# Row-factor root, rotary steps and weight sums reordered in front of the attention loop of a hybrid decoder block

## The chip, the cores and the metric

The kernel runs on one core of a Trainium2 chip. That core has five engines with a queue of instructions each: TensorE (PE) for matrix products, VectorE (DVE) and ScalarE (ACT) for element-wise work, GpSimd (POOL) for element-wise work on the core's own memory and for issuing transfers, and SyncE (SP) for issuing transfers. An engine takes its instructions in the order of its queue; the engines meet at semaphores. PE writes to the accumulator memory PSUM, which is divided into banks.

The metric is the device time of one execution in microseconds (us), from the first to the last work of the program; lower is better.

## The reference

One layer on x of 1024 rows by 1024 channels, all in float32. An RMS norm is followed by a projection into a pooling input u (512), 8 query heads and 2 key/value heads of 64, and two gates of 1024. The first 16 channels of each query and key head are rotated by position. Attention runs in blocks of 128 rows over the block itself and the one before, with a window of 128 and one sink logit per head. A multi-scale average pooling with its own mixing is the other branch. Both go through branch weights, are gated and added, and an output projection, a norm and a squared-ReLU MLP follow.

```python
h = _rmsnorm(x, g_mix_pre[l])
proj = jnp.einsum('bsd,de->bse', h, w_in[l]) + b_in[l]
u_pool, q, k, v, gates = jnp.split(proj, IN_SPLITS, axis=-1)
y_pool = _multiscale_pool(u_pool, w_pool[l], pool_scale[l])
q = _partial_rotary(q.reshape(B, S, N_Q_HEADS, HEAD_DIM), cos, sin)
k = _partial_rotary(k.reshape(B, S, N_KV_HEADS, HEAD_DIM), cos, sin)
...
y_attn = _sliding_window_sink_attention(q.reshape(...), k, v, attn_sinks[l])
merged = (g_pool * jnp.einsum('bsc,cd->bsd', y_pool, w_branch_pool[l])
          + g_attn * jnp.einsum('bsc,cd->bsd', y_attn, w_branch_attn[l]))
mix = jnp.einsum('bsd,de->bse', merged, w_out[l])
x = x + _rmsnorm(mix, g_mix_post[l])
```

## The kernel before

**Number format.** Every float32 operand of a product is split into a high part (a rounding copy, mostly on ACT, L101) and a low part (the difference, on DVE, L104); a product is three matmuls, high by high, high by low and low by high. So each operand costs one ACT and one DVE instruction before PE can use it whole.

**The front.** Channels lie on partitions and the 1024 rows are cut into two halves of 512 (`th` 0 and 1). The six groups of 128 projected channels are f = 0 to 3 (queries with 32 value channels each) and f = 4, 5 (the first 80 partitions hold the channels to be rotated, in two halves; the rest keys that are not). For each of 8 slices k of the input channels, `scaled` multiplies x by the norm's gain (high part on ACT at L202, low on DVE at L203), and `mm_in` (L187) adds three matmuls. The norm's factor per row, r1, comes from sums of squares: `square_row` (and L967 for the second half) squares a tile of rows on ACT and sums along it into `ssq`; `factors` takes a root on ACT and a Newton step on DVE through `rsqrt` and spreads the result (L218); `make_rb` transposes it on PE (L224) and copies it as the row `rb` (L225). `close_in` multiplies a finished projection by `rb` on DVE (L353) and adds its bias on ACT (L354). The buffers of the closed second half are those of the first, so the close at f = 4 waits until the first half's rows have been copied out.

**Rotation.** `turn` multiplies the 80 rows by a cosine and a sine table (two instructions of 80x1024, L363), `turn_end` takes their difference and sum (L367, L368), and `rows_in`, `keys_rest` and `values_out` send the rows by small transfers to where queries, keys and values need them, over the queues of SP, ACT and POOL. The first half's rotation runs on DVE, the second's on POOL, in `second_half`, which is what `closing` holds and `flush(closing)` runs.

**Attention.** For each block n of 128 rows: `split_q` makes the query operands (`qt`), `score_all` the scores in two groups of heads (L456) with a copy on ACT (L458), `score_prev` masks them on DVE (L465), `softmax_max` takes maxima (L472 to L474), `softmax_exp` eight exponentials on ACT (L480, L482), `softmax_scale` divides on DVE (L486 to L488), `attend_t` transposes the probabilities on PE (L499) and splits them, `attend_own` masks a copy on DVE (L508), and `attend_v` multiplies by the values (L524) and copies the result (`yt`, L526). Scores, transposes and outputs share two double banks ("sc"), so each waits until the one before last has been read.

**The filler.** The order on PE, DVE and ACT is the order of the program text. Between the steps of attention `fill(t)` takes steps from a stream (`others`) of products that have nothing to do with the block: first 48 steps of the second half's projection (8 for each f), then 16 half products of the gates (L643) of four steps each, with four products of branch weights (`wb_mm`, L780) of two steps in between. A step is three matmuls and is counted as 3 x 0.227 us. `fill` keeps what it has overdrawn and takes whole steps. What the stream needs (splits of gate weights, `load_wb`'s scaled branch weights at L765 on ACT and L768 on DVE) is put on the other engines when the stream reaches certain steps, through the lists `between`, `due` and `lazy`; so where `fill` stands also decides where those instructions stand on ACT and DVE. The stream ends with block 7; whatever the fills took earlier is not there later.

**Weight sums.** `presum(h)` forms sums of parts of the attention branch's weights on DVE, two instructions of 128x512 at each of its two calls (L309, L310; then L305, L306), and stores them for a later stage.

Lines in this text and in the prediction are those of the kernel before, if not said otherwise; the order of the changed kernel shows its own line numbers, which are up to 13 higher (10 in most cases).

Of the kernel before, what the change touches and what calls it, by code (L numbers as in the profile page):

```python
# [8 lines left out]
F32 = mybir.dt.float32  # L9
F32R = mybir.dt.float32r  # L10
# [40 lines left out]
def block_kernel(ctx: ExitStack, tc, xt, x, consts, vecs, sinks, rot, g_post, g_mlp, g_mlp_post,  # L51
# [152 lines left out]

    ssq = sp.tile([P, 20 * NT], F32, name="ssq", bufs=1)[:, :NT]

# [5 lines left out]
    tv = bcp.tile([P, 1024], F32, tag="bc", name="tv")  # L212

    def factors(th):
        n = slice(4 * th, 4 * th + 4)
        rsqrt(r1[:, n], ssq[:, n], 4)
        t = rows_of[th] = at("s4", 4, [2, 512])[:, 0, :]
        dve.tensor_copy(t.rearrange("p (n k) -> p n k", k=P), r1[:, n].unsqueeze(2).broadcast_to([P, 4, P]))  # L218
# [16 lines left out]
    with tc.manual_schedule(engines={mybir.EngineType.PE}):  # L235
# [40 lines left out]
        for n in range(4):  # L276
            square_row(n, at("qkv", 3, [S]) if n < 3 else at("s4", 4, [S]))
        load_table(0)
        factors(0)
        for k in range(NK):  # L280
            if k % 2 == 0:
                xs = flat(yy.tile([P, 2, 512], F32, tag="y", name=nm("xs")))
            nc.sync.dma_start(xs[:, k % 2 * 512:(k % 2 + 1) * 512], xt[k][:, 512:])
            if k < 4:
                scaled(k, 1, xs[:, k % 2 * 512:(k % 2 + 1) * 512])
            else:
                x_late.append((k, 1, xs[:, k % 2 * 512:(k % 2 + 1) * 512]))
# [69 lines left out]

    def turn(th, eng):

        t, tab = raw_r[th][:NR], tables.pop(th)  # L360
        turned[th] = [at("s4", 4, [2, 512])[:NR] for _ in range(2)]
        for i, o in enumerate(turned[th]):
            eng.tensor_tensor(o, t, tab[:NR, i, :].unsqueeze(1).broadcast_to([NR, 2, 512]), ALU.mult)  # L363
# [53 lines left out]
    def second_half(f):  # L417
        close_in(f, 1)
        if f == 5:
            keys_rest(nc.gpsimd, 1)  # L420
            turn(1, pool)
            turn_end(1, pool)
            rows_in(nc.gpsimd, 1, raw_k[1], 4)
        elif f < 4:
            values_out(nc.gpsimd, 1, f)
# [526 lines left out]
    with tc.manual_schedule(engines={mybir.EngineType.PE, mybir.EngineType.DVE, mybir.EngineType.Activation}):  # L952
# [5 lines left out]
        close_in(5, 0)  # L958
        scaled(*x_late[0])
        turn(0, dve)  # L960
        keys_rest(nc.sync, 0)
        for x_ in x_late[1:]:
            scaled(*x_)
        turn_end(0, dve)
        rows_in(nc.sync, 0, raw_k[0], 4)
        for n in range(4, NT):
            act.activation(squares_late[n], squares_late[n], AF.Square, accum_out=ssq[:, n:n + 1])  # L967
        for m in range(4):
            close_in(m, 0)
        factors(1)  # L970
        for m, q in enumerate((nc.sync, nc.sync, nc.scalar, nc.gpsimd)):
            rows_in(q, 0, raw_of(m, 0), m)
        for m in range(4):
            values_out(nc.gpsimd, 0, m)
        load_table(1)
        fill(8.8)
        make_rb(1)
        ready[0] = True
        act.activation(warm, r1[:, :1], AF.Exp)
        flush(closing)  # L980
        presum(0)
        presum(0)
        dve.tensor_scalar(nsnk, snk, -1.0, None, ALU.mult)
        split_k(0)
        fill(3.4)
        split_q(0)
        fill(1.4)
        score_all(0)
        act.activation(tv[:, :512], tv[:, :512], AF.Identity, bias=vec[:, V_BV:V_BV + 1])
        score_prev(0, 0)  # L990
        score_prev(0, 1)
        softmax_max(0)
        split_q(1)
        fill(2.2)
        post_v(0)
        wps = stage([4, P])
        nc.sync.dma_start(wps, w_pool)
        presum_load(1)
        softmax_exp(0, range(3))
# [8 lines left out]
        softmax_max(1)  # L1008
        wpt = yy.tile([P, 2, 4, P], F32R, tag="y", name="wpt")
        split(wpt[:, 0], wpt[:, 1], wps)  # L1010
        wpts.append(wpt)
        fill(3.7)
        for n in range(NT):
            attend_t(n)
            attend_own(n)
            if n == 0:
                presum(1)
            flush(due[0])
# [1507 lines left out]
```

## Time and profile before

| | us |
|---|---|
| three runs, median (lowest to highest) | 1109.07 (1108.18 to 1109.65) |
| the profiled execution's own time | 1108.53 |
| its span, first to last instruction | 1106.7 |
| TensorE busy | 1082.6 (98%) |
| VectorE busy | 901.2 (81%) |
| ScalarE busy | 647.1 (58%) |
| GpSimd busy | 111.2 (10%) |
| mean granted TensorE clock | 0.992 of full |

The profile is of one execution. The span is divided into stretches in which different engines set the pace, and the shares above are means over all of them. In rows of the timeline the columns are start, length, engine, line, operation, output and inputs by the program's names, shapes and count; a bracket at the end is idle time just before, with the instruction that ended it. "PE" are matmuls, "ACTq" is ScalarE's queue when it issues a transfer. Between 0 and about 39 us PE works through the first half's projection, from there to about 183 us through filler and attention, and behind it through gates, branches, output projection and MLP.

### The profile page before, as it was taken

What the parts mean: (1) busy time and instruction counts of PE and PEld (TensorE: products, weight loads), DVE (VectorE), ACT (ScalarE), POOL (GpSimd) and SP (SyncE); (2) the same over time, 40 slices, a digit from 0 to 9 for tenths busy, and PEclk for the clock granted to TensorE, in tenths of its full rate; (3) what the DMA queues carried; (4) which work ended last, traced back from release to release, by engine and by line L of the source; (5) the groups of instructions that cost most, each with busy time, mean ns of one, the idle gap of its engine ahead of it and who ended that gap; (6) DMA issues with size and microseconds to landing.
All of it is one profiled execution on the core that took longest, in us unless ns stands there. A gap on an engine that the chain in (4) does not pass through costs nothing.

```text
span 1106.7 us, 14808 instructions
## 1 busy us (share of the span) xinstructions
PE 1082.6 (98%) x5247; PEld 904.6 (82%) x5247; DVE 901.2 (81%) x1300; ACT 647.1 (58%) x1084; POOL 111.2 (10%) x170
## 2 busy tenths in 40 slices
PE   9997899999999999999999999999999999999997
PEld 7776677888888888888888888888888899899886
DVE  5687789999979787879987976766666899899997
ACT  6757686656665226777765655555544375265653
POOL 0155332200000001100000000100100000000000
PEclk9999899999999999999999999999999999999999
DMA  8747769967994876833276855564898777549842
GB/s 296 230 129 200 201 168 273 295 205 248 298 266 143 232 224 133 237 126 133 96 265 248 292 187 196 182 229 159 279 402 276 240 247 269 169 154 340 296 151 76
DMA packets 107657, 243.30 MB, mean 220 GB/s; under 512 B 10816, under 2 KB 28480, under 8 KB 107584
## 3 DMA queue, kind: packets, MB, share of 16 engines
q1 hardware_dynamic: 86576, 191.76, 51.0%
q0 software_dynamic: 15040, 30.48, 11.5%
q10 hardware_dynamic: 5968, 20.12, 4.7%
q8 instruction: 41, 0.67, 0.2%
q14 instruction: 32, 0.26, 0.1%
HBM read 166.30 MB, written 73.40 MB: 217 GB/s over the span
## 4 chain that ended last, share of the span: by engine, by line
PE 82%; DVE 5%; ACT 3%; issue 2%; DMA 1%; POOL 0%; DVEq 0%; SPq 0%; ACTq 0%
PE mm L643 24%; PE at L643 16%; PE at L2211 12%; PE mm L2211 5%; PE mm L1605 5%; PE at L2185 4%; PE mm L2185 4%; PE mm L554 3%; PE at L1605 2%; PE at L1333 2%; PE mm L1333 1%; PE mm L556 1%; PE sc L524 1%; DVE s L508 1%; ACT s L482 1%
## 5 line engine op out<-in xcount | busy, mean ns | idle before, releaser
L2211 PE MATMUL at<-ar,wh 128*128 128x512 f32 x564 | 134.6, 389 | 0.0
L2211 PEld LDWEIGHTS at<-ar,wh 128*128 128x128 f32 x564 | 105.8, 188 | 22.2 <-DVE ar L104 0.3
L104 DVE TENSOR_TENSOR wh<-st,wh 128x512 fp32r<-128x512 f32 (+1 forms) x106 | 76.3, 731 | 29.7 <-ACT wh L101 27.1
L101 ACT CAST wh<-raw 128x1024 fp32r<-128x1024 f32 (+1 forms) x54 | 53.3, 988 | 79.8 <-PE at L2211 51.9
L643 PE MATMUL mm<-T,wx 128*128 128x512 f32 x375 | 90.6, 389 | 0.0
L104 DVE TENSOR_TENSOR wh<-raw,wh 128x1024 fp32r<-128x1024 f32 (+1 forms) x54 | 61.7, 1142 | 29.6 <-ACT wh L101 29.1
L643 PEld LDWEIGHTS mm<-T,wx 128*128 128x128 f32 x375 | 70.3, 188 | 14.8 <-DVE wx L104 0.2
L101 ACT CAST wh<-st 128x512 fp32r<-128x512 f32 (+2 forms) x105 | 67.6, 653 | 17.7 <-DVE st L599 5.8
L643 PE MATMUL mm<-gr,wh 128*128 128x512 f32 x321 | 77.4, 391 | 0.0
L643 PEld LDWEIGHTS mm<-gr,wh 128*128 128x128 f32 x321 | 59.9, 188 | 12.1
L2211 PE MATMUL mm<-ar,wh 128*128 128x512 f32 x276 | 69.5, 389 | 0.0
L643 PE MATMUL mm<-T,wh 128*128 128x512 f32 x267 | 66.0, 389 | 0.0
L643 PE MATMUL mm<-x,wh 128*128 128x512 f32 x240 | 60.8, 402 | 2.0 <-DVE wh L104 1.2
L101 ACT CAST ar<-B 128x1024 fp32r<-128x1024 f32 (+2 forms) x59 | 43.0, 757 | 30.7 <-PE mm L2211 14.8
L2211 PEld LDWEIGHTS mm<-ar,wh 128*128 128x128 f32 x276 | 51.8, 188 | 10.7
L643 PE MATMUL at<-gr,wh 128*128 128x512 f32 x243 | 59.1, 390 | 0.1
L643 PEld LDWEIGHTS mm<-T,wh 128*128 128x128 f32 x267 | 50.1, 188 | 10.4
L643 PEld LDWEIGHTS mm<-x,wh 128*128 128x128 f32 x240 | 45.6, 194 | 12.8 <-DVE wh L104 1.6
L643 PEld LDWEIGHTS at<-gr,wh 128*128 128x128 f32 x243 | 45.5, 188 | 9.9 <-ACT g L651 0.5
L643 PE MATMUL at<-T,wx 128*128 128x512 f32 x213 | 52.2, 389 | 0.0
L104 DVE TENSOR_TENSOR ar<-B,ar 128x1024 fp32r<-128x1024 f32 (+2 forms) x59 | 49.1, 857 | 1.1 <-ACT ar L101 1.1
L2185 PE MATMUL at<-ar,wh 128*128 128x256 f32 x336 | 47.5, 283 | 0.0
(565 smaller groups left out, 2491.3 us busy)
## 6 DMA issues: line engine op xcount, KB each, us to landing
raw<-f_dram SPq DMA_DIRECT2D x40, 512.0 KB, 4.0
B<-in_w_dn_dram SPq DMA_DIRECT2D x32, 512.0 KB, 6.9
st<-in_w_up_dram SPq DMA_DIRECT2D x27, 512.0 KB, 4.5
f_dram<-g SPq DMA_DIRECT2D x21, 512.0 KB, 3.2
wh<-f_dram SPq DMA_DIRECT2D x20, 512.0 KB, 4.3
g<-spill_dram SPq DMA_DIRECT2D x17, 512.0 KB, 6.6
st<-in_w_g_dram SPq DMA_DIRECT2D x16, 512.0 KB, 4.4
f_dram<-g ACTq DMA_DIRECT2D x16, 512.0 KB, 2.6
```

What stands on the lines that cost most here:

```text
L101: act.copy(hi, src)
L104: return eng.tensor_tensor(lo, src, f32(hi), ALU.subtract)
L482: act.activation(s8[:, h], s8[:, h], AF.Exp, scale=SCALE, bias=nmx[:, h:h + 1], accum_out=den[:, h:h + 1])
L508: dve.tensor_tensor(t, f32(s), own_t.unsqueeze(1).broadcast_to([P, NH, P]), ALU.mult)
L524: pe.matmul(yb[:, kv], v[:, c:c + P], p[ph][:, 4 * kv:4 * kv + 4].rearrange("p i q -> p (i q)"), start=j < 2, stop=j >= len(mms) - 2)
L554: pe.matmul(bs[th], whi[:, k, :], rhs(k, hl, th), start=k == 0 and hl == 0, stop=False)
L556: pe.matmul(bs[th], wlo[:, k, :], rhs(k, 0, th), start=False, stop=k == nk - 1)
L643: pe.matmul(b, w[wh][:, kt, :], x_, start=not after and kt == 0 and j == 0, stop=kt == 3 and j == 2, skip_group_check=after)
L1333: pe.matmul(b, w[wh][:, kt, :], xo[xh][:, kt, :], start=not after and kt == 0 and j == 0, stop=kt == 1 and j == 2, skip_group_check=after)
L1605: pe.matmul(bs[t], Am[a][k][ah][:, t * P:(t + 1) * P], Wm[w][k][wh], start=not after and k == 0 and j == 0, stop=k == 3 and j == 2, skip_g ...
L2185: pe.matmul(part[q][:, t, :], o[fs][fh][:, fk, t * P:(t + 1) * P], o[ws][wh][:, wk, :], start=q not in onto and (s_, t, j) == (0, 0, 0), s ...
L2211: pe.matmul(bs[t], fo[fh][:, k2, t * P:(t + 1) * P], wo_[wh][:, k2, :], start=not after and s2 == 0 and k2 == 0 and j == 0, stop=(s2, k2) ...
```

## The change

Five things are done, all between 36 us and the loop over the blocks:

- The root of the row factors is taken out of `rsqrt` into `root(th)`, which stands right behind the squares on ACT; `factors` keeps the Newton step on DVE. For the second half `factors(1)` now stands behind the four closes and the row transfers. (`ssq` gives up some of its unused room.)
- In the front six instead of four `scaled` of the second half come ahead of `make_rb(0)`. The first rotation's second multiply goes from DVE to POOL.
- The second rotation leaves `second_half` and POOL: `turn(1, dve, dve)`, `turn_end(1, dve)` and `rows_in` stand behind block 0's `softmax_max`, together with the split of `w_pool`, which stood ahead of the loop.
- Both calls of `presum(0)`, the Exp table's warm-up and the sink's negation come ahead of the first `fill`; `split_k(0)` comes ahead of `flush(closing)`; `presum(1)`'s first call moves from block 0 in the loop to the end of the front.
- The fills in front of the loop are 10.8 and 4.3 where there were 8.8, 3.4 and 1.4.

```diff
+    def root(th):
+        roots[th] = small(4, "root")
+        act.activation(roots[th], ssq[:, 4 * th:4 * th + 4], AF.Sqrt, scale=1.0 / D, bias=eps)
...
     def factors(th):
         n = slice(4 * th, 4 * th + 4)
-        rsqrt(r1[:, n], ssq[:, n], 4)
+        ms, r, t = (small()[:, :4] for _ in range(3))
+        dve.tensor_scalar(ms, ssq[:, n], 1.0 / D, EPS, ALU.mult, ALU.add)
+        dve.reciprocal(r, roots.pop(th))
...
         load_table(0)
+        root(0)
         factors(0)
...
-            if k < 4:
+            if k < 6:
                 scaled(k, 1, xs[:, k % 2 * 512:(k % 2 + 1) * 512])
...
         if f == 5:
             keys_rest(nc.gpsimd, 1)
-            turn(1, pool)
-            turn_end(1, pool)
-            rows_in(nc.gpsimd, 1, raw_k[1], 4)
...
-        scaled(*x_late[0])
-        turn(0, dve)
+        turn(0, dve, pool)
         keys_rest(nc.sync, 0)
-        for x_ in x_late[1:]:
+        for x_ in x_late:
             scaled(*x_)
         turn_end(0, dve)
         rows_in(nc.sync, 0, raw_k[0], 4)
         for n in range(4, NT):
             act.activation(squares_late[n], squares_late[n], AF.Square, accum_out=ssq[:, n:n + 1])
+        root(1)
         for m in range(4):
             close_in(m, 0)
-        factors(1)
...
+        factors(1)
         load_table(1)
-        fill(8.8)
+        presum(0)
+        presum(0)
+        act.activation(warm, r1[:, :1], AF.Exp)
+        dve.tensor_scalar(nsnk, snk, -1.0, None, ALU.mult)
+        fill(10.8)
         make_rb(1)
         ready[0] = True
-        act.activation(warm, r1[:, :1], AF.Exp)
+        split_k(0)
         flush(closing)
-        presum(0)
-        presum(0)
-        dve.tensor_scalar(nsnk, snk, -1.0, None, ALU.mult)
-        split_k(0)
-        fill(3.4)
         split_q(0)
-        fill(1.4)
+        wps = stage([4, P])
+        nc.sync.dma_start(wps, w_pool)
+        presum_load(1)
+        fill(4.3)
         score_all(0)
...
         softmax_max(0)
+        wpt = yy.tile([P, 2, 4, P], F32R, tag="y", name="wpt")
+        split(wpt[:, 0], wpt[:, 1], wps)
+        wpts.append(wpt)
+        turn(1, dve, dve)
+        turn_end(1, dve)
+        rows_in(nc.gpsimd, 1, raw_k[1], 4)
         split_q(1)
...
         softmax_max(1)
-        wpt = yy.tile([P, 2, 4, P], F32R, tag="y", name="wpt")
-        split(wpt[:, 0], wpt[:, 1], wps)
-        wpts.append(wpt)
+        presum(1)
         fill(3.7)
         for n in range(NT):
             attend_t(n)
             attend_own(n)
-            if n == 0:
-                presum(1)
             flush(due[0])
```

More of the change, by code (lines that the diff above doesn't have):

```diff
@@ L203, in scaled @@
         dve.scalar_tensor_tensor(t[:, 1, a:b], xs[:, a:b], gk, f32(t[:, 0, a:b]), ALU.mult, ALU.subtract)
-    ssq = sp.tile([P, 20 * NT], F32, name="ssq", bufs=1)[:, :NT]
+    ssq = sp.tile([P, 17 * NT], F32, name="ssq", bufs=1)[:, :NT]
     def square_row(n, t):
@@ L212, in block_kernel @@
     tv = bcp.tile([P, 1024], F32, tag="bc", name="tv")
+    roots = {}
+    def root(th):
+        roots[th] = small(4, "root")
+        act.activation(roots[th], ssq[:, 4 * th:4 * th + 4], AF.Sqrt, scale=1.0 / D, bias=eps)
     def factors(th):
         n = slice(4 * th, 4 * th + 4)
-        rsqrt(r1[:, n], ssq[:, n], 4)
+        ms, r, t = (small()[:, :4] for _ in range(3))
+        dve.tensor_scalar(ms, ssq[:, n], 1.0 / D, EPS, ALU.mult, ALU.add)
+        dve.reciprocal(r, roots.pop(th))
+        dve.tensor_tensor(t, r, r, ALU.mult)
+        dve.tensor_tensor(t, t, ms, ALU.mult)
+        dve.tensor_scalar(t, t, -0.5, 1.5, ALU.mult, ALU.add)
+        dve.tensor_tensor(r1[:, n], r, t, ALU.mult)
         t = rows_of[th] = at("s4", 4, [2, 512])[:, 0, :]
@@ L356, in block_kernel, with turn @@
     turned, raw_k = {}, {}
-    def turn(th, eng):
+    def turn(th, *engs):
         t, tab = raw_r[th][:NR], tables.pop(th)
         turned[th] = [at("s4", 4, [2, 512])[:NR] for _ in range(2)]
-        for i, o in enumerate(turned[th]):
+        for i, (o, eng) in enumerate(zip(turned[th], engs)):
             eng.tensor_tensor(o, t, tab[:NR, i, :].unsqueeze(1).broadcast_to([NR, 2, 512]), ALU.mult)
@@ L995, in block_kernel @@
         post_v(0)
-        wps = stage([4, P])
-        nc.sync.dma_start(wps, w_pool)
-        presum_load(1)
         softmax_exp(0, range(3))
```

## The prediction

> **What bounds the kernel now.** The page comes first, with the busy time of each engine and its share of the span of 1106.7 us.
>
> ```profile
> PE 1082.6 (98%) x5247; PEld 904.6 (82%) x5247; DVE 901.2 (81%) x1300; ACT 647.1 (58%) x1084; POOL 111.2 (10%) x170
> ```
>
> TensorE (PE) works 98% of the span, so only its idle time can be won, and that is not spread evenly. Next the stretches (start:end, then length, busy time of PE, its weight loads, VectorE, ScalarE, GpSimd, granted clock, DMA share, GB/s):
>
> ```profile
> 30.00:60.00 30.00, 26.01 (x132) 20.71 (x131) 20.54 (x42) 19.91 (x36) 4.49 (x9) 0.98 0.70 228
> 60.00:90.00 30.00, 26.32 (x149) 20.51 (x148) 24.21 (x34) 17.04 (x56) 20.24 (x31) 0.96 0.40 114
> 90.00:130.00 40.00, 34.10 (x175) 26.60 (x174) 28.43 (x42) 27.01 (x77) 15.33 (x24) 0.91 0.78 219
> 130.00:183.00 53.00, 50.56 (x280) 40.14 (x279) 48.69 (x65) 44.10 (x114) 18.81 (x31) 0.99 0.75 201
> 183.00:1107.00 924.00, 916.67 (x4391) 772.78 (x4389) 764.52 (x1092) 519.77 (x770) 51.04 (x69) 1.00 0.67 222
> ```
>
> The idle of 30 to 183 us is 3.99 + 3.68 + 5.90 + 2.44 = 16.0 us; all that the diff touches lies there. Behind 183 us PE is full up to its last matmul, so what has shifted by then shifts the end. Who PE waited for (total us, times, longest):
>
> ```profile
> PE mm L780 <- ACT wh L765: 2.8, 1, 2.8
> PE mm L224 <- DVE s L218: 1.8, 1, 1.8
> PE sc L456 <- DVE klo L104: 1.5, 1, 1.5
> PE sc L456 <- DVE qt L104: 1.4, 3, 0.6
> PE mm L187 <- DVE x L203: 0.7, 1, 0.7
> ```
>
> The change aims at L203, L224 and L104's klo: 0.7 + 1.8 + 1.5 = 4.0 us in front of the loop. The waits in the loop, L780 above all, are not touched by a line of the diff, but by its order.
>
> The marks that I measure by are starts on PE: filler of the second half, first scores, transposes of block 0 and of block 1, the second gate half's low weights, the first L780 product's low half, a plain run of filler, the last transposes, and the first matmul behind the loop.
>
> ```profile
> 38.73 3.79 PE L187 MATMUL mm<-x,wkv 128*128 128x512 f32 x16
> 57.54 0.33 PE L456 MATMUL sc<-klo,qt 64*128 64x128 f32 x2 [1.46 <-DVE klo L104]
> 74.11 1.06 PE L499 MATMUL sc<-cst,s 128*128 128x128 f32 x8 [0.36 <-DVE s L488]
> 88.56 1.09 PE L499 MATMUL sc<-cst,s 128*128 128x128 f32 x8 [1.85 <-DVE s L465]
> 97.19 1.20 PE L643 MATMUL mm<-x,wh 128*128 128x512 f32 x4 [1.17 <-DVE wh L104]
> 114.51 2.07 PE L780 MATMUL mm<-wh,wpt 128*128 128x512 f32 x4 [1.11 <-DVE wh L768]
> 150.26 5.72 PE L643 MATMUL mm<-x,wh 128*128 128x512 f32 x24
> 176.15 1.03 PE L499 MATMUL sc<-cst,s 128*128 128x128 f32 x8
> 182.80 3.40 PE L643 MATMUL mm<-x,wh 128*128 128x512 f32 x9
> ```
>
> A filler step is three matmuls: 24 in 5.72 us make 0.7 us a step (0.68 by the kernel's own figure).
>
> **The change part by part.** Prices of VectorE (DVE), in order: two multiplies of the first rotation, one of its sums, two masked copies and a maximum's scaling beside GpSimd, q's two low parts beside GpSimd, the copies alone, a maximum and its scaling alone, one weight sum (a projection's close has its width, 128x512), and a weight's low part that waited for ACT.
>
> ```profile
> 40.16 2.35 DVE L363 TENSOR_TENSOR s<-qkv,s 80x1024 f32<-80x1024 f32 x2
> 45.02 0.69 DVE L368 TENSOR_TENSOR qkv<-s,s 80x512 f32<-80x512 f32 x1
> 59.93 3.54 DVE L465 COPY_PREDICATED s<-cst,pad 128x512 f32<-128x512 uint32 x2 [1.26 <-ACT s L458]
> 64.76 0.96 DVE L473 SCALAR_TENSOR_TENSOR nmx<-nmx,nsnk 128x8 f32<-128x8 f32 x1
> 65.88 1.84 DVE L104 TENSOR_TENSOR qt<-qkv,qt 128x256 fp32r<-128x256 f32 x2
> 69.58 1.37 DVE L465 COPY_PREDICATED s<-cst,sc 128x512 f32<-128x512 uint32 x2 [1.26 <-ACT s L458]
> 73.89 1.21 DVE L472 TENSOR_REDUCE nmx<-s 128x8 f32<-128x1024 f32 x1
> 75.13 0.17 DVE L473 SCALAR_TENSOR_TENSOR nmx<-nmx,nsnk 128x8 f32<-128x8 f32 x1
> 77.51 0.68 DVE L309 TENSOR_TENSOR st<-st,st 128x512 f32<-128x512 f32 x1
> 85.84 0.69 DVE L104 TENSOR_TENSOR wh<-st,wh 128x512 fp32r<-128x512 f32 x1 [2.22 <-ACT wh L101]
> ```
>
> And GpSimd's two multiplies of the second rotation:
>
> ```profile
> 60.33 5.37 POOL L363 TENSOR_TENSOR s<-qkv,s 80x1024 f32<-80x1024 f32 x2
> ```
>
> ScalarE (ACT): row copies issued, `rb` copied, the Exp table, block 0's cast, the copy of its attention output, a branch weight scaled.
>
> ```profile
> 48.98 1.87 ACTq L375 DMA_DIRECT2D qkv<-qkv  x2
> 51.31 0.58 ACT L225 COPY rb_all<-mm 128x512 f32<-128x512 f32 x1 [2.22 <-PE mm L224]
> 51.91 1.28 ACT L979 ACT_TABLE_LOAD   x1
> 75.25 1.01 ACT L101 CAST s<-sc 128x1024 fp32r<-128x1024 f32 x1 [2.63 <-POOL dv L104]
> 83.69 0.99 ACT L526 COPY yt<-sc 128x1024 f32<-128x1024 f32 x1
> 111.47 1.15 ACT L765 ACTIVATE wh<-st,vec 128x1024 fp32r<-128x1024 f32 x1
> ```
>
> *In front of the first scores.* Two `scaled` go ahead of the wait for `rb`, where ACT and DVE stand idle: the 0.7 goes. Half of the first rotation goes to GpSimd at 5.37 / 2 = 2.7 us or a little less, since the two rows of L465 show DVE and GpSimd delaying each other; DVE saves 2.35 / 2 = 1.2, waits, and is done with L368 about 0.7 earlier (45.0 for 45.7). The root behind the squares takes its wait out of `factors`, so the row factors are ready at about 49; sixteen steps of filler from 38.73 end at 49.7, and the 1.8 goes. But `rb` doesn't come earlier: ACT ends its row copies at 50.85 - 0.7 = 50.1, and now loads the table and warms it up (1.28 + 0.2) before it copies `rb`: 51.6 to 52.2, where before had 51.9. Then the keys are split ahead of the closes: 0.6 on ACT (the width of L225), 0.7 on DVE, a close on DVE and two on ACT (0.7 + 1.2), the first of q's casts of half the width (0.3), 0.3 for hand-overs: first scores at about 56.0, 1.5 earlier. PE has 16 + 7 steps done at 54.9, three more than before had, and waits 1.1 there.
>
> *The second rotation on DVE.* It costs 2.35 + 2 x 0.69 = 3.7 us. It saves 3.54 - 1.37 = 2.2 and 0.96 - 0.17 = 0.8 that the two engines took from each other, and 1.84 - 2 x 0.35 = 1.1 at q's low parts (half the width of a 0.69), which stood beside GpSimd's sums: 4.1 together. So it pays for itself, little more; the 1.5 is left and block 0's transposes start at about 72.7, when its probabilities are scaled, with two more steps of filler done.
>
> *The weight sums.* Here the order decides. ACT before, from the eight transposes' neighbours on (q is the projection that is closed, s_119 block 0's probabilities):
>
> ```order
> L407 COPY tv<-mm_759 128x128
> L101 CAST wpt<-st_691 128x512
> L101 CAST s_119_802<-sc_804 128x1024
> L480 ACTIVATE es_773<-es_773 128x8
> L482 ACTIVATE s_107_717,den_774<-s_107_717,nmx_772 128x128 x8
> ```
>
> ACT now, at the same place:
>
> ```order
> L420 COPY tv<-mm_771 128x128
> L367 ACTIVATE q_716<-q_716,vec 128x512
> L101 CAST s_119_816<-sc_818 128x1024
> L490 ACTIVATE es_785<-es_785 128x8
> L492 ACTIVATE s_107_729,den_786<-s_107_729,nmx_784 128x128 x8
> ```
>
> A close of ACT, which needs DVE's close, has come ahead of the cast. DVE before, from block 0's scaling on:
>
> ```order
> L488 TENSOR_TENSOR s_93_629<-s_93_629,den_663 128x1024
> L472 TENSOR_REDUCE nmx_772<-s_107_717 128x8
> L473 SCALAR_TENSOR_TENSOR nmx_772<-nmx_772,nsnk 128x8
> L474 TENSOR_TENSOR es_773<-snk,nmx_772 128x8
> L104 TENSOR_TENSOR wpt<-st_691,wpt 128x512
> L104 TENSOR_TENSOR s_120_803<-sc_804,s_119_802 128x1024
> ```
>
> And now:
>
> ```order
> L498 TENSOR_TENSOR s_94_637<-s_94_637,den_671 128x1024
> L482 TENSOR_REDUCE nmx_784<-s_107_729 128x8
> L483 SCALAR_TENSOR_TENSOR nmx_784<-nmx_784,nsnk 128x8
> L484 TENSOR_TENSOR es_785<-snk,nmx_784 128x8
> L322 TENSOR_TENSOR st_610<-st_609,st_610 128x512
> L323 TENSOR_TENSOR st_609<-st_609 128x512
> L366 TENSOR_TENSOR q_716<-mm_695,rb_all 128x512
> L104 TENSOR_TENSOR s_120_817<-sc_818,s_119_816 128x1024
> ```
>
> That close stands behind the maximum (1.21 + 2 x 0.17 = 1.6) and the two sums (1.4), and the low part of wpt has gone to an earlier place. The cast starts at 72.7 + 1.6 + 1.4 + 0.7 + 0.6 = 77.0 instead of 75.25, 1.75 later. Queued behind it on ACT are block 1's exponentials, q's casts, the next close and a weight's cast, and only then block 0's output copy, which frees the bank of the second half of block 2's scores: 83.69 + 1.75 + 0.6 (the weight's cast, which stood behind it) = 86.0. PE waits some 3 us there. DVE gives the 1.75 back, because it had 2.22 to wait at L104's low part (85.84): block 2's masked copies, block 1's transposes (88.56) and the second half's low weights (97.19) come when they came before. The lead is gone.
>
> *The filler.* `fill` in front of the loop grows from 22.7 to 24.2, two steps. At 97.2 both kernels have done the same filler, but the new one has two steps more to do before block 3's scores: 2 x 0.68 = 1.4 later, and with them the chain of ACT and DVE up to L768: the product at about 115.9. PE idles for it, so behind it the two steps count again: 1.4. Two more waits come from scaled branch weights (ACT 1.15 each) that now stand ahead of a block's score copies. The scores themselves take PE, by the chain,
>
> ```profile
> 120.96 1.65 PE sc L456 x20
> ```
>
> From block 2's last attention product on, ACT has the output copy (0.9), the weight (1.15), a cast (0.6), the first score copy (0.5), and DVE the masked copy (0.7): 3.9 with hand-overs 4.1. PE has two steps (1.4), block 4's scores (1.65) and no more filler ahead of block 3's transposes: a wait of about 1.0. At block 6 DVE's half of the weight stands in the way too (1.2, as ACT's), and PE has a step more (0.7): about 1.0 again, taking 0.5 off for work of ACT that is done by then. On the other side the two longer waits for q's low parts (1.0 of the 1.4) find their cover. At the end, PE before:
>
> ```order
> L643 MATMUL mm_1871<-x_335,wh_1749 128x512 x3
> L499 MATMUL sc_1893<-cst,s_278_1702 128x128 x8
> L780 MATMUL mm_1911<-wh_1821,wpt 128x512 x2
> L780 MATMUL mm_1911<-wh_1822,wpt 128x512
> L780 MATMUL mm_1912<-wh_1821,wpt 128x512 x2
> L780 MATMUL mm_1912<-wh_1822,wpt 128x512
> L524 MATMUL sc_1931<-s_310_1891,v_1575 128x512 x2
> ```
>
> And now:
>
> ```order
> L653 MATMUL mm_1871<-x_335,wh_1749 128x512 x3
> L790 MATMUL mm_1890<-wh_1821,wpt 128x512 x2
> L790 MATMUL mm_1890<-wh_1822,wpt 128x512
> L790 MATMUL mm_1891<-wh_1821,wpt 128x512 x2
> L790 MATMUL mm_1891<-wh_1822,wpt 128x512
> L509 MATMUL sc_1907<-cst,s_281_1715 128x128 x8
> L534 MATMUL sc_1931<-s_313_1905,v_1594 128x512 x2
> ```
>
> The last two steps (L790) have moved ahead of the last transposes, which nothing covers now. From those to 182.80 lies 6.65 us of cast, split and masks, and it stays; so the end moves as the last transposes do.
>
> *Sum.* 0 (lead given back) + 1.4 + 1.4 + 1.0 + 1.0 - 1.0 = 3.8 us. The profiled execution took 1108.5 (1106.7 of span, the rest around it), 0.5 under the median of the runs, 1109.1: so 1112.3 in its own terms, and 1112.9 on the median.
>
> *The clock.* Two stretches with idle time of PE, clock in the third column from the end:
>
> ```profile
> 85.00:90.00 5.00, 3.15 (x27) 2.48 (x26) 4.08 (x6) 2.27 (x6) 4.25 (x11) 1.00 0.77 196
> 115.00:120.00 5.00, 5.00 (x13) 3.84 (x13) 0.76 (x2) 1.78 (x4) 0.20 (x1) 0.50 0.98 322
> ```
>
> The wait of 1.9 left the clock at 1.00; those of 2.8 and 1.1 brought 0.50. My walk has some 3 us at block 2's scores, and at the second gate half's weights 97.2 - 92.6 = 4.6 less what their high part covers (88.3 + 0.8 of transposes + 5 steps of 0.7 is 92.6): each place may bring a dip. The bounds are 0 and half of a 5 us stretch, 2.5, each; I take 0 in the sum, since the wait of 1.9 is the nearest single one, and keep the rest for a rival. [...]
>
> **The rivals.**
> - *The clock gives the waits a price* (0.15): both new places bring a dip. For it, the row of 0.50; against it, that part of a dip falls on waits. At the middle of its bounds, 1.25 each, it gives 1112.9 + 2.5 = 1115.4. [...]
> - *A wash* (0.25): block 0's cast isn't held as long, the lead of 1.5 reaches L780's product, and the later waits eat it: -1.5 + 1.0 + 1.0 - 1.0 = -0.5, that is 1108.6. For it, that DVE has 5.8 us of idle time between 60 and 90 to catch up in (24.2 of 30 busy).
> - *Faster* (0.12): DVE, no longer held up by GpSimd, is so quick that ACT's order never bites. The point that decides is the start of block 0's cast: under 74 us the front gain of 1.5, the wait at L499 (1.9) and those for q's low parts (1.0) are won, against two new waits of 1.0: 1109.1 - 2.4 = 1106.7. Against it, the close stands behind 3.7 us of DVE work.
> - *The forecast* (0.48): 1112.9.
>
> **How the numbers follow.** 0.2% of 1109.1, about what a measurement tells from no change, is 2.2 us: same is 1106.9 to 1111.3. The forecast's five terms, each wrong by half and on their own, make 1.3; the lead at the low weights is unsure by some 2: together 1110.5 to 1115.3, of which a sixth is still same. Slower: 0.41 from the forecast, 0.15 from the clock, 0.06 from the wash's upper edge, 0.62. Same: 0.07 + 0.17 = 0.24. Faster: 0.12 and the wash's lower edge, 0.02: 0.14. The range runs from 1107.0, which takes in the wash, to 1117.0, which takes in the clock's case with a dip of 2 each.
>
> **What would show it.** In the changed profile: no wait at L187 and at the second `rb` transposes; first scores near 56.0, with PE waiting for q's cast; block 0's transposes near 72.7, its cast near 77; a wait of some 3 us on the copy of yt at block 2's scores; the first L780 product's low half near 115.9; waits on masked copies in front of block 3's and block 5's transposes; last transposes near 180, with nothing between them and the last attention product. I am wrong if the cast starts by 75, or if the first product's low half starts before 114.

## The result, and the profile after

The changed kernel takes 1113.82 us (median of 6 runs, 1112.21 to 1114.69), the kernel before beside it 1108.72 (6 runs): the ratio is 1.0044, 95% interval 1.0031 to 1.0057. It is slower by 5.1 us in the medians. The profiled execution of the changed kernel took 1112.21 with a span of 1110.4, 3.7 over the span of before. It was the fastest of the six (the next took 1113.51), so what follows is read from an execution that lost less than the median one. The forecast had 1112.9, and 1110.5 for the end of the span.

First the engines' busy time on the page of the changed kernel.

```profile
PE 1083.1 (98%) x5247; PEld 906.7 (82%) x5247; DVE 898.8 (81%) x1303; ACT 647.2 (58%) x1084; POOL 105.9 (10%) x167
```

As before, 98%: the loss has to be looked for in the stretches, cut as in the prediction.

```profile
30.00:60.00 30.00, 29.13 (x149) 23.83 (x148) 21.78 (x43) 21.80 (x40) 9.49 (x10) 1.00 0.76 242
60.00:90.00 30.00, 23.33 (x124) 18.45 (x124) 21.12 (x35) 14.65 (x50) 11.06 (x21) 0.87 0.30 81
90.00:130.00 40.00, 31.90 (x156) 24.43 (x156) 23.83 (x36) 24.15 (x65) 11.96 (x24) 0.84 0.70 203
```

In front of 60 us PE gained 3.1 us of work (29.13 for 26.01). Between 60 and 130 it lost 5.2 (55.23 for 60.42), which leaves it 2.1 us less busy by 130, and the granted clock there fell from 0.96 and 0.91 to 0.87 and 0.84. What PE waited for, in the changed kernel:

```profile
PE mm L790 <- ACT wh L775: 3.9, 1, 3.9
PE sc L466 <- DVE qt L104: 3.8, 2, 2.5
PE sc L466 <- ACT yt L536: 2.9, 1, 2.9
...
PE mm L653 <- ACT wh L101: 1.7, 1, 1.7
```

The waits that the change aimed at (L203, `rb`, klo) are gone. In their place stand q's low parts (2.46 at block 1's scores, 1.36 at block 2's), the copy of `yt`, the gate weights and the product's weight. The marks on PE, in the order of the prediction (start, length, line, shape, and the wait ahead):

```profile
55.69 0.33 PE L466 MATMUL sc<-klo,qt 64*128 64x128 f32 x2 [0.74 <-ACT qt L101]
...
72.94 1.07 PE L509 MATMUL sc<-cst,s 128*128 128x128 f32 x8
87.20 0.58 PE L466 MATMUL sc<-klo,qt 64*128 64x256 f32 x2 [2.85 <-ACT yt L536]
90.43 1.92 PE L509 MATMUL sc<-cst,s 128*128 128x128 f32 x8
99.82 4.67 PE L653 MATMUL mm<-x,wh 128*128 128x512 f32 x13 [1.33 <-DVE wh L104]
119.42 2.07 PE L790 MATMUL mm<-wh,wpt 128*128 128x512 f32 x4 [0.31 <-DVE wh L778]
129.70 1.09 PE L509 MATMUL sc<-cst,s 128*128 128x128 f32 x8 [0.79 <-DVE s L475]
155.97 1.09 PE L509 MATMUL sc<-cst,s 128*128 128x128 f32 x8 [1.06 <-DVE s L475]
181.81 1.03 PE L509 MATMUL sc<-cst,s 128*128 128x128 f32 x8
```

And on ScalarE, the close that came ahead, block 0's cast, and the copy of its output:

```profile
76.59 0.72 ACT L367 ACTIVATE q<-q,vec 128x512 f32<-128x512 f32 x1 [5.65 <-DVE q L366]
77.22 0.99 ACT L101 CAST s<-sc 128x1024 fp32r<-128x1024 f32 x1
86.14 1.00 ACT L536 COPY yt<-sc 128x1024 f32<-128x1024 f32 x1
```

| start, us | before | forecast | changed |
|---|---|---|---|
| first scores | 57.54 | 56.0 | 55.69 |
| block 0's transposes | 74.11 | 72.7 | 72.94 |
| block 0's cast | 75.25 | 77.0 | 77.22 |
| copy of its output | 83.69 | 86.0 | 86.14 |
| block 1's transposes | 88.56 | 88.3 | 90.43 |
| low weights, second gate half | 97.19 | 97.2 | 99.82 |
| first product's low half | 114.51 | 115.9 | 119.42 |
| last transposes | 176.15 | near 180 | 181.81 |
| end of the span | 1106.7 | 1110.5 | 1110.4 |

Up to the output's copy every mark is within 0.3 us of the forecast. Then comes a break: against the forecast block 1's transposes are 2.1 us late, the low weights 2.6 and the product 3.5. At its end the sum is right again, so something was also gained that the forecast didn't have. The clock (third column from the end), in stretches of 5 us, shows where the break starts:

```profile
85.00:90.00 5.00, 2.80 (x15) 2.38 (x16) 3.12 (x5) 3.21 (x5) 1.52 (x3) 0.59 0.34 66
90.00:95.00 5.00, 5.00 (x22) 4.26 (x22) 3.62 (x6) 2.88 (x12) 3.38 (x7) 0.73 0.77 259
100.00:105.00 5.00, 5.00 (x16) 3.99 (x17) 2.27 (x4) 1.82 (x3) 0.56 (x1) 0.71 1.01 344
120.00:125.00 5.00, 5.00 (x16) 3.94 (x15) 0.76 (x2) 1.78 (x4) 0.18 (x1) 0.66 1.00 282
180.00:185.00 5.00, 3.58 (x19) 2.54 (x17) 4.81 (x7) 4.58 (x8) 0.00 (x0) 1.00 0.84 234
```

In stretches of half a microsecond from 84 to 126 the clock reads 1.00 or 0.50, but for those in which it changes. So 0.59 and 0.73 are 4.1 and 2.7 us at half clock, one piece from about 85.9 to 92.7 (0.50 over the whole of it), in which the scores and transposes behind the wait of 2.85 run; the transposes take 1.92 for 1.09. A second piece follows the waits at the gate weights (0.51 in 99.5 to 103.0), a third the product's (0.50 in 116.6 to 123.4). (An earlier one, 0.66 in 65 to 70, follows the wait of 2.46 at block 1's scores; the marks behind it are on time.) The last row stands for the end of the loop: full clock, where the kernel before has 0.69.

### The profile page after: what moved, and what is told of

Read it like the earlier page. It is cut to its first block, busy times and chain, and to the rows that moved or that the text cites. A ratio compares the mean times of both kernels' runs of the same rounds, so it can differ in the third digit from the quotient of the medians.

```text
span 1110.4 us, 14797 instructions
## 1 busy us (share of the span) xinstructions
PE 1083.1 (98%) x5247; PEld 906.7 (82%) x5247; DVE 898.8 (81%) x1303; ACT 647.2 (58%) x1084; POOL 105.9 (10%) x167
## 4 chain that ended last, share of the span: by engine, by line
PE 89%; DVE 5%; ACT 4%; issue 1%; DMA 0%; DVEq 0%; SPq 0%; ACTq 0%
PE mm L653 25%; PE at L653 18%; PE at L2222 12%; PE mm L2222 5%; PE mm L1616 5%; PE at L2196 4%; PE mm L2196 4%; PE mm L564 3%; PE sc L187 2%; PE at L1616 2%; PE at L1344 2%; PE mm L187 2%; PE mm L1344 1%; PE mm L566 1%; PE sc L534 1%
## 5 line engine op out<-in xcount | busy, mean ns | idle before, releaser
L2222 PEld LDWEIGHTS mm<-ar,wh 128*128 128x128 f32 x276 | 51.8, 188 | 10.8
```

Of the source, the lines that this page charges most:

```text
L2222: pe.matmul(bs[t], fo[fh][:, k2, t * P:(t + 1) * P], wo_[wh][:, k2, :], start=not after and s2 == 0 and k2 == 0 and j == 0, stop=(s2, k2) ...
```

## The experiments

The first theory is the forecast's: the close of f = 1 on ACT gives the front's lead back, and two steps of filler, done ahead of the loop, are missing later. Two rivals: the loss is in the granted clock, or in the rotation on VectorE. All results in one table; each difference is taken to the median of the kernel before that ran beside it, since that moved from 1108.37 to 1109.17. The intervals of two rows together are about 2 us either way, so a smaller difference between two rows is not shown.

| run | median | before | difference | ratio, 95% |
|---|---|---|---|---|
| changed kernel | 1113.82 | 1108.72 | +5.1 | 1.0031 to 1.0057 |
| e1, close later | 1110.14 | 1108.39 | +1.8 | 1.0006 to 1.0024 |
| e2, fill back (34 steps) | 1105.24 | 1108.39 | -3.2 | 0.9959 to 0.9987 |
| e3, sums back | 1112.31 | 1108.39 | +3.9 | 1.0024 to 1.0048 |
| e4, rotation on GpSimd | 1115.75 | 1108.39 | +7.4 | 1.0054 to 1.0083 |
| e5, before with 36 steps | 1114.09 | 1108.37 | +5.7 | 1.0040 to 1.0065 |
| e6, busy waits | 1111.30 | 1108.37 | +2.9 | 1.0013 to 1.0037 |
| e7, busy waits, fill back | 1105.24 | 1108.37 | -3.1 | 0.9965 to 0.9990 |
| e8, 32 steps | 1111.30 | 1108.37 | +2.9 | 1.0012 to 1.0033 |
| e9, front only | 1109.32 | 1109.17 | +0.2 | 0.9996 to 1.0014 |
| e10, rotation only | 1108.50 | 1109.17 | -0.7 | 0.9983 to 1.0003 |
| e11, 33 steps | 1104.43 | 1109.17 | -4.7 | 0.9950 to 0.9977 |
| e12, rotation later | 1102.78 | 1109.17 | -6.4 | 0.9932 to 0.9957 |

### The order alone (e1)

```diff
-                if k == 2 and ready[0]:
+                if k == (4 if f == 2 else 2) and ready[0]:
                     flush(closing)
```

> The changed kernel, with the close of the query group f = 1 (L366 on VectorE, L367 on ScalarE) put two filler steps later, so that it stands behind block 0's cast and split as in the kernel before; the filler and everything else stay. First theory (the forecast's: this order gives the front's lead back, and the two filler steps cost 1.4 us twice): block 0's cast starts near 75.4 us for 77.2, the copy of its output near 84.4 for 86.1, the wait at block 2's scores falls from 2.85 to about 1.1, and the time falls by 1.5, to 1112.3. Rival (the loss is in the granted clock): with that wait the half clock of 85.9 to 92.7 us goes or is cut to one piece, and the time falls by 3 or more, to 1110.8 or less. Rival (the rotation on VectorE is the loss, since block 1's scores wait 2.46 us for q's low part): no change, 1113.8.

PE's marks in this run, and ACT's cast:

```profile
84.44 0.39 PE L466 MATMUL sc<-klo,qt 64*128 64x256 f32 x2 [1.99 <-ACT yt L536]
...
93.23 0.91 PE L653 MATMUL mm<-x,wh 128*128 128x512 f32 x2 [2.46 <-ACT wh L101]
95.08 5.73 PE L653 MATMUL mm<-x,wh 128*128 128x512 f32 x13 [0.94 <-DVE wh L104]
115.78 2.07 PE L790 MATMUL mm<-wh,wpt 128*128 128x512 f32 x4 [0.32 <-DVE wh L778]
```
```profile
73.83 1.02 ACT L101 CAST s<-sc 128x1024 fp32r<-128x1024 f32 x1 [3.85 <-PE sc L509]
```

One close, two steps later, is worth 3.3 us (5.1 - 1.8), not 1.5: the cast starts 3.4 earlier, the low weights 4.7. The half clock behind block 2's scores is gone (1.00 in 85 to 90). But another has come behind the gate weights, where the wait for the high part has grown from 1.74 to 2.46 (the stretches of 90 to 95, 95 to 100 and 100 to 105):

```profile
90.00:95.00 5.00, 1.68 (x6) 0.60 (x4) 4.93 (x9) 4.38 (x18) 1.24 (x2) 0.86 0.85 243
95.00:100.00 5.00, 4.92 (x12) 3.86 (x13) 2.52 (x5) 1.90 (x4) 1.61 (x2) 0.50 0.84 274
100.00:105.00 5.00, 5.00 (x39) 3.98 (x38) 0.04 (x1) 1.94 (x3) 1.94 (x5) 0.95 0.96 297
```

The profiled execution of e1 took 1111.6, 1.5 over its median, and its span (1109.8) is only 0.6 under that of the changed kernel: it met half clock at the end of the loop (0.74 and 0.58 in 180 to 190), where the profile of the changed kernel has none. So the 3.3 stands on the medians, and the marks show the way only as far as the product. Order and clock can't be told apart in this run; e6 does that in part. The rotation wasn't touched, and the time fell: it is not the whole loss.

### The filler (e2, e8, e11, and e5 on the kernel before)

e2 (34 steps), e11 (33) and e8 (32) change the last fill of the changed kernel; e5 gives the kernel before 36.

```diff
-        fill(3.7)
+        fill(2.2)
```

> The changed kernel with the last fill in front of the loop at 2.2 for 3.7: the loop begins with 34 steps of filler done, as in the kernel before, for 36; that also takes the close of f = 1 behind block 0's cast. First theory: the order's 1.5 and the filler's 1.4 + 1.4 come back, 1113.8 - 4.3 = 1109.5; the first product's low half near 115.5 for 119.4. Rival (clock): the waits ahead of the loop become longer by what filler is missing there, block 1's transposes keep a wait over 1.5 us, and only 1.5 comes back: 1112.3. Rival (rotation): no change, 1113.8.

```profile
72.48 1.07 PE L509 MATMUL sc<-cst,s 128*128 128x128 f32 x8 [0.88 <-DVE s L498]
...
93.61 0.73 PE L653 MATMUL mm<-x,wh 128*128 128x512 f32 x2 [0.83 <-ACT wh L101]
95.46 1.20 PE L653 MATMUL mm<-x,wh 128*128 128x512 f32 x4 [1.12 <-DVE wh L104]
113.39 2.07 PE L790 MATMUL mm<-wh,wpt 128*128 128x512 f32 x4 [1.23 <-DVE wh L778]
```

With the same filler as before, the change makes the kernel faster, by 3.2 us. Taking the two steps and the order back is worth 8.3 us, where the expectation had 4.3; without the order (e1 to e2) the two steps are worth 4.9, where it had 2.8. The waits at the gate weights (0.83 and 1.12) bring no half clock now (1.00 from 90 to 105), and block 3's and block 5's transposes wait no more for masked copies.

```diff
-        fill(3.7)
+        fill(5.2)
```

> The kernel before with its last fill in front of the loop at 5.2 for 3.7, and nothing else: 36 steps of filler ahead of the loop for 34, which also puts the close of f = 1 ahead of block 0's cast. If filler and order have the price that the two runs on the changed kernel gave them (1113.8 - 1105.2 = 8.6 us together), wherever they stand, this takes 1108.4 + 8.6 = 1117.0. The forecast's prices (1.75 for the order, 1.4 + 1.4 for the filler) give 1108.4 + 4.5 = 1112.9. Rival (the two only cost beside the rest of the change, in whose lead the order bites): 1108.4 to 1110.

The result, +5.7, is between the prices, nearer to the forecast's. So two steps more cost 5.7 us on the kernel before and 8.3 on the changed one. Read the other way: at 36 steps all the rest of the change is worth 0.6 us, which can't be told from nothing, at 34 steps 3.2. The filler's amount hides what the rest brings.

```diff
-        fill(3.7)
+        fill(0.8)
```

> The changed kernel with the last fill in front of the loop at 0.8: 32 steps ahead of the loop, four under the changed kernel and two under the run with the fill back (1105.2 us). If each pair of steps costs what the last did without the order, 4.9 us (1110.1 - 1105.2), this takes 1100.3. If filler ahead of the loop is good as long as it stands in a wait, then at block 0's transposes, which wait 0.9 at 34 steps, PE waits 1.4 more for the chain, nothing is won up to the low weights, and only the later 1.4 comes back: 1103.8. Rival (two steps less leave waits without cover): 1105 to 1107.

All three expectations fell: +2.9, 6.1 us worse than 34 steps. ScalarE around the first product's weight (L775):

```profile
117.27 0.40 ACT L101 CAST qt<-s 128x256 fp32r<-128x256 f32 x1 [2.60 <-DMA s<-qkv]
...
118.49 1.15 ACT L775 ACTIVATE wh<-st,vec 128x1024 fp32r<-128x1024 f32 x1
```

With 32 steps the product comes behind block 2's attention product, and its weight on ACT behind q's cast, which waits 2.60 for a transfer of rows. At 34 steps L775 stood ahead of both and started at 109.74.

```diff
-        fill(3.7)
+        fill(1.5)
```

> The changed kernel with the last fill in front of the loop at 1.5: 33 steps, between 34 (1105.2 us) and 32 (1111.3). If the loss at 32 comes with the first product's moving behind block 2's attention product on TensorE, it hangs on which step that takes: with the product still ahead, 1104.5 (0.7 less); with it behind, 1110 to 1111. If the loss grows evenly with the waits, 1108.

-4.7: as good as 34 steps or better. Half of the product is still ahead of the attention product, L775 starts at 111.79, ahead of q's casts. So the loss does not grow evenly with the missing filler. Up to the low weights of the second gate half, 32 steps are 1.1 us behind 33 (96.27 for 95.20); most of the difference comes behind them, where the order tips. Half clock is in it too (0.50 and 0.83 in 95 to 105 at 32 steps, 0.66 and 1.00 at 33), and no run parts the two.

### The clock (e6, e7)

```diff
+    def keep_busy(b, n, start=False):
+        for _ in range(n):
+            pe.matmul(b, zeros[:, :P], zeros, start=start, stop=start)
...
         bs = [bank("mm") for _ in range(2)]
+        if gi == 3:
+            keep_busy(bs[0], 10, True)
...
+            if (n, g) == (2, 1):
+                keep_busy(b_in[3, 1], 10)
             score(n, g)
...
+        if (p, i) == (8, 2):
+            keep_busy(b, 6, True)
         for kt in range(4):
```

> The changed kernel, with matmuls of zeros on TensorE where it waits: ten (2.3 us at full clock) ahead of the second half of block 2's scores, six (1.4) ahead of the second gate half, ten ahead of the first product. They add zero to an open sum, or write a bank that the next matmul overwrites. If the granted clock is the loss (rival), the half clocks of 85.9 to 92.7, 99.5 to 103.0 and 116.6 to 123.4 us go, 17 us at half speed, of which a third fell on waits: some 6 us back, about 1108. If the loss is in the waits themselves (forecast), the clocks change little in time, within 1.5 us: 1112.3 to 1114.

The marks again, and the zeros (L186) ahead of block 2's second scores:

```profile
83.66 2.45 PE L186 MATMUL mm<-const-float32-0.0 128*128 128x512 f32 x10
...
88.40 1.08 PE L515 MATMUL sc<-cst,s 128*128 128x128 f32 x8
97.21 4.61 PE L659 MATMUL mm<-x,wh 128*128 128x512 f32 x13 [1.12 <-DVE wh L104]
116.76 1.72 PE L800 MATMUL mm<-wh,wpt 128*128 128x512 f32 x4 [0.80 <-DVE wh L786]
```

The clock rows of the same run for 85 to 95:

```profile
85.00:90.00 5.00, 4.53 (x33) 3.52 (x32) 4.27 (x6) 3.37 (x7) 2.59 (x6) 1.00 0.40 78
90.00:95.00 5.00, 4.23 (x19) 3.21 (x17) 4.86 (x9) 4.64 (x21) 2.32 (x5) 1.00 0.82 250
```

Work that computes nothing makes the kernel 2.2 us faster. The low weights start at 97.21 for 99.82, 2.6 us earlier. Of these, 0.6 was there ahead of the zeros (PE's scores ahead of them start at 82.88 for 83.49, ACT's copy at 85.53 for 86.14). From the copy to the low weights e6 takes 11.68 us, the changed kernel 13.68: these 2.0 us are the half clock behind block 2's scores, and most of the break in the table of marks. That 88.40 and 97.21 are the forecast's 88.3 and 97.2 is luck in part, since the copy is half a microsecond ahead of the forecast's 86.0. The gain was expected at 6 us by the clock's side and under 1.5 by the other; 2.2 lies between: the piece of half clock behind the gate weights stayed (0.67 in 95 to 100), and half of the product's (0.72 and 0.94 in 115 to 125).

On e2, with the same ten zeros ahead of the product and eight ahead of block 1's scores:

```diff
+            if (n, g) == (1, 0):
+                keep_busy(b_in[1, 1], 8)
             score(n, g)
```

> The run with the fill back (1105.2 us) and matmuls of zeros in its waits that are followed by half clock: eight (1.8 us) ahead of block 1's scores, ten (2.3) ahead of the first product. Rival (clock): the half clocks from 65.4 and from 112.8 us go, 10.3 us in all, and with them up to 5, less what falls on waits: 1101.5. Forecast's side (the chain of ScalarE and VectorE sets the next waits, so PE is only idle in another place): the first goes and changes nothing before the transposes of block 0, the second gives about 1.5: 1103.7.

No gain, and both sides had expected one. The half clock moved from 65 to 70 us (0.66 there in e2) into the next two stretches, and the wait went with it:

```profile
65.00:70.00 5.00, 4.66 (x35) 3.61 (x35) 2.69 (x6) 3.75 (x14) 2.31 (x6) 1.00 0.13 26
70.00:75.00 5.00, 2.30 (x12) 2.11 (x12) 4.82 (x8) 0.82 (x2) 3.67 (x7) 0.83 0.08 16
```
```profile
72.72 1.43 PE L515 MATMUL sc<-cst,s 128*128 128x128 f32 x8 [2.70 <-DVE s L504]
```

Ahead of block 0's transposes PE waits 2.70 for DVE's scaling now, for 0.88 in e2: PE was ahead of the chain there, and time that it gains is time that it waits.

### The sums and the rotation (e3, e4, e9, e10, e12)

```diff
-        presum(1)
         fill(3.7)
...
             attend_own(n)
+            if n == 0:
+                presum(1)
```

> The changed kernel with the first two weight sums of the second part (two subtractions and additions of 128x512 on VectorE, 1.4 us) back in block 0 of the loop, behind its split; the close of f = 1 stays ahead of the cast, but no longer behind the sums. First theory: the cast comes 1.4 earlier, near 75.8, the wait at block 2's scores falls to about 1.5, and the time falls by 1.0 to 1.4, to about 1112.6; less than in the run that moves the close, because the sums now stand on VectorE in front of block 1's scaling. Rival (clock): by 2.5 or more where the half clock at 85.9 is cut, else 1113.0. Rival (rotation): no change, 1113.8.

1.2 us back by the medians, as the first theory had it, but less than two rows of the table can show. The cast starts at 75.97 (expected 75.8) and the copy of its output is 1.25 earlier; the wait at block 2's scores, expected at 1.5, stayed at 2.85. So the run fits the first theory, and doesn't rule out that the sums cost nothing.

```diff
             keys_rest(nc.gpsimd, 1)
+            turn(1, pool, pool)
+            turn_end(1, pool)
+            rows_in(nc.gpsimd, 1, raw_k[1], 4)
...
         wpts.append(wpt)
-        turn(1, dve, dve)
-        turn_end(1, dve)
-        rows_in(nc.gpsimd, 1, raw_k[1], 4)
```

> The changed kernel with the second rotation (two multiplies, a difference and a sum) and its row transfers back on GpSimd, in the second half's closing, as in the kernel before; the rest stays. First theory (the rotation on VectorE pays for itself, 4.1 us saved for 3.7): no change within 1 us, 1112.8 to 1114.8; the masked copies of block 0 go back to 3.5 us for two and q's low parts to 1.8, and block 1's scores wait about 0.5 for 2.46. Rival (rotation): the wait at block 1's scores was the loss, and the time falls by 2 to 2.5, to about 1111.5. Rival (clock): no half clock at 65.4 us, so 1.7 less, about 1112.1.

All three fell: 2.3 us slower. The rotation on VectorE isn't the loss; in this kernel it is a gain. Then the same edit at 34 steps (e9, with this beside it):

```diff
-        fill(3.7)
+        fill(2.2)
```

> The run with the fill back (34 steps ahead of the loop, 1105.2 us), with the second rotation back on GpSimd in the closing: against the kernel before only the front is changed. The forecast held that the rotation on VectorE saves 4.1 us for 3.7: 1105.2 + 0.4 = 1105.6. With the price of the run that put it back on GpSimd at 36 steps (1115.8 - 1113.8 = 1.9): 1107.1. If the rotation is what won the 3.1 us at 34 steps, and the front nothing: 1108.4.

And the rotation alone, on the kernel before, taken out of `second_half` as in the change (e10):

```diff
         softmax_max(0)
+        turn(1, dve)
+        turn_end(1, dve)
+        rows_in(nc.gpsimd, 1, raw_k[1], 4)
         split_q(1)
```

> The kernel before with the second rotation on VectorE behind block 0's maximum, and nothing else of the change (34 steps). By the forecast's prices 1108.4 - 0.4 = 1108.0; by the price found at 36 steps, 1106.5; if the rotation was all that won, 1105.2. Together with the run of the front alone it shows whether the two gains add.

Neither alone gains what can be told from nothing (+0.2 and -0.7), and both together gain 3.2. VectorE and GpSimd in the run with the front only show what the front lacks alone:

```profile
55.94 5.44 DVE L104 TENSOR_TENSOR qt<-qkv,qt 128x256 fp32r<-128x256 f32 x2 [1.15 <-ACT qt L101]
56.43 4.66 POOL L376 TENSOR_TENSOR s<-qkv,s 80x1024 f32<-80x1024 f32 x2
```

The front puts q's low parts where GpSimd's two multiplies of the rotation begin. One of the two 128x256 subtractions takes 0.42 us, the other 5.10, about as long as the multiplies last (4.66); PE waits 4.13 for it, half clock follows (0.50 in 60 to 65), and block 0's transposes start at 76.05 instead of 72.48 as in e2. Without the front (e10) the rotation on VectorE pushes block 0's cast from 75.25 to 76.61. So each of the two moves loses in one place what the other would win there; that this is all of it was not tested.

Last, a version that follows from the traces. In e2, ACT stood idle 4.47 us for the close of f = 0, which DVE did behind the rotation; block 1's score copies and five exponentials were queued behind it.

```diff
-        turn(1, dve, dve)
-        turn_end(1, dve)
-        rows_in(nc.gpsimd, 1, raw_k[1], 4)
         split_q(1)
...
         fill(2.5)
+        turn(1, dve, dve)
+        turn_end(1, dve)
+        rows_in(nc.gpsimd, 1, raw_k[1], 4)
         score_all(1)
```

> The run with the fill back (1105.2 us), with the rotation on VectorE moved behind q's low parts and the close of f = 0, still ahead of block 1's masks. ScalarE stood idle 4.5 us for that close, with block 1's score copies and five of block 0's exponentials queued behind it. If that order sets block 0's transposes, the wait of 2.55 at block 1's scores goes, block 0's scaling ends near 69.5 for 72.3, its transposes start near 70 for 72.5, and with the filler as it is the time falls by about 2, to 1103.2. If the rotated keys then come too late for block 2's scores, or what is won there is given back at the first product, 1105.2.

VectorE in this run, and PE's transposes of block 0:

```profile
62.07 0.68 DVE L366 TENSOR_TENSOR q<-mm,rb_all 128x512 f32<-128x512 f32 x1
62.67 2.34 DVE L376 TENSOR_TENSOR s<-qkv,s 80x1024 f32<-80x1024 f32 x2
...
67.91 1.23 DVE L498 TENSOR_TENSOR s<-s,den 128x1024 f32<-128x1024 f32 x1
```
```profile
69.28 1.06 PE L509 MATMUL sc<-cst,s 128*128 128x128 f32 x8 [1.75 <-DVE s L498]
```

As expected: the wait at block 1's scores is gone, the scaling ends at 69.1, and the time is 1102.78, 0.9945 of the kernel before (0.9932 to 0.9957). This version beats both kernels.

## Why the prediction was right or wrong

**Right: the sign, and the path up to block 2's scores.** First scores, transposes, cast and copy came within 0.3 us, the wait on `yt` was 2.85 for "some 3", the waits on masked copies 0.79 and 1.06 for 1.0 each, and the two waits for q's low parts that were to find cover (0.36 and 0.64) are gone. e1 shows that the order of close and cast is a cause, as the forecast said, with more than its price (3.3 for 1.75); e3 fits, but is too small to decide.

**Wrong: "DVE gives the 1.75 back", the lead of 0 at the low weights, and with it the clock's term of 0.** The low weights came 2.6 late, and e6 shows that the half clock behind block 2's scores is 2.0 of that. DVE did have the slack: block 1's transposes have no wait for it. But PE ran the scores at half clock, and so reached the transposes 2 us later. The clock was a rival at 0.15 and 1.25 us a dip; it came, and in this place cost more.

**Too small: the filler up to the product, 1.4.** From the low weights to the product's low half the changed kernel takes 19.60 us, before 17.32, e2 17.93: 1.7 for the two steps against e2, and 0.6 that comes with the rest of the change. The half clock of 100 to 105 (0.71) may be part of it; in e6 that piece stayed, and so did the time (19.55 us), so no run shows its price.

**Wrong: "behind it the two steps count again: 1.4".** At the first product's low half both kernels have the same work left, 4744 matmuls, so nothing counts again. The stretch from there to the end, before and changed:

```profile
114.51:1106.70 992.19, 982.72 (x4744) 825.47 (x4744) 821.06 (x1167) 572.72 (x906) 73.40 (x104) 0.99 0.67 220
119.42:1110.40 990.98, 979.72 (x4744) 823.77 (x4744) 819.89 (x1167) 572.53 (x906) 72.63 (x104) 1.00 0.68 221
```

The changed kernel is 1.2 us faster there, where the forecast had it 2.4 slower. PE is idle 1.8 us more (11.26 for 9.47): the forecast's 0.79 + 1.06 - 1.0, and a wait of 1.15 for the last block's cast, which the last two steps covered before. But the same matmuls take 3.0 us less, and up to 2.6 of that is clock. Behind the product's weight the kernel before runs at half clock up to about 120.5, 6.0 us from the low half on (0.50 in 114.5 to 120.5), the changed one up to 123.4, 4.0 us (0.50 in 119.4 to 123.4): up to 1.0. And at the end of the loop the kernel before had this (changed kernel: 1.00, shown above):

```profile
180.00:185.00 5.00, 4.17 (x12) 2.80 (x11) 4.97 (x6) 3.12 (x4) 1.03 (x1) 0.69 1.01 305
```

0.69 is 3.1 us at half clock, up to 1.6 us, which the changed kernel didn't meet in its profiled execution. The other runs with 36 steps met it there in their profiles (e1, e3, e4, e5), but for e6. No term of the forecast had either.

So the sum, 3.8 for 3.7 in the profiled executions, is closer than its parts: 3.5 us too little ahead of the product, and behind it 3.6 too much, by a term counted twice (1.4), and by 3.0 of matmul time, most of it clock, less 0.8 of waits that the forecast lacked. By the medians the loss is 5.1. The forecast's mechanism was right up to block 2's scores; behind them its arithmetic was helped by luck.

**Not seen: what hung on the filler.** The forecast gave its two steps 2.8 us and the order the lead of 1.5; together they were worth 8.3. The rival *faster* had named the right point, block 0's cast under 74 us. e2 puts it at 73.59 and takes 1105.2, where that rival had 1106.7. The term "it pays for itself, little more" for the rotation fits on the kernel before (-0.7 for -0.4, neither of which can be told from nothing), but not in the changed one, where the rotation on GpSimd falls on q's low parts (e9). Its place was not priced either: behind block 0's maximum it holds up the close of f = 0, and PE waits 2.46 at block 1's scores; at 34 steps e12 wins 3.2 us there.

Open stays how much of the 4.9 us from e1 to e2 is clock and how much is missing cover: e1 has 6.9 us of half clock behind the low weights that e2 hasn't, and no run held the clock up there with the order as in e1.

## What to carry to other kernels

Where an order is written out and a stream of filler carries other engines' work along, a change of the filler's amount changes orders too: try it apart from the moves it comes with, since here it hid a gain of 3.2 us behind a loss of 8.3. Before a lead is counted, follow the strict order of the in-between engines (here ScalarE) to the first instruction that waits for another engine, and ask what is queued behind it: moving one close, or the rotation behind one close, was worth 3 us each time. Price waits of PE of some 2.5 us, alone or two close together, with the half clock that followed most of them here (0.66 in the stretch behind 2.46 in the changed kernel, 0.59 behind 2.85, 0.50 behind 2.46 and 0.94 in e1), and give work that VectorE and GpSimd held each other up in (5.10 us for 0.42 in e9) a place where nobody waits for either.

## What the runs showed of the hardware

- One 128x256 subtraction on VectorE took 5.10 us beside GpSimd's two multiplies (e9), and 0.42 alone. The other way round, GpSimd's 80x1024 multiply took 4.76 us in the first rotation (the forecast had 2.7, from 5.37 for two), while VectorE's multiply beside it took 1.22, about as alone (2.35 for two in the kernel before). VectorE was busy there with the multiply and two low parts (L203) until 41.36. An estimate from these rows: with 2.33 for the multiply, half of the 4.66 that two took in e9, and nothing done before 41.36, GpSimd would end at 43.69, and it ended at 43.63. So GpSimd was held up in the one place, VectorE in the other. In both VectorE's instruction is recorded as the first to start (38.82 and 56.30 against 38.87 and 56.43), so the recorded starts don't tell which of the two is held up.

```profile
38.82 1.22 DVE L376 TENSOR_TENSOR s<-qkv,s 80x1024 f32<-80x1024 f32 x1 [0.81 <-ACT qkv L367]
38.87 4.76 POOL L376 TENSOR_TENSOR s<-qkv,s 80x1024 f32<-80x1024 f32 x1 [37.08 <-DMA snk<-in_sinks_dram]
```

- The same short waits bring half clock in one kernel and none in another: at the end of the loop, waits of 0.5, 0.5 and 0.3 us in before (0.69 in 180 to 185) and in e2 (1.00). What decides it was not shown. Half clock followed a single wait of 2.85 us in the changed kernel (0.59 in 85 to 90) and waits of 1.74 and 1.33 close together (0.71 in 100 to 105); behind a wait of 1.85 in the kernel before, and of 1.99 in e1, the clock stayed at 1.00.
- Half clock in the middle of a chain cost less than half its length here: of the piece from 85.9 to 92.7, 6.8 us, 2.0 us show at the low weights, and e6 took away some 10 us of half clock in all (17 to 7 in 85 to 125) and won 2.2. In e7 it cost nothing that the medians show: the piece at block 1's scores moved behind a wait of 2.70 for VectorE, the one behind the product's weight is 3.3 us shorter than in e2 (3.5 for 6.8 in 110 to 120), and the median is 1105.24 in both.
